# RWKV state update in a two-layer hybrid trunk: both heads' products on the same 64 partitions, and one VectorE instruction that writes the state

## Chip, cores and metric

The kernel runs on one core of one Trainium2 chip. The metric is the device time of one execution in microseconds, the median of the runs shown; smaller is better.

## What is computed

The program is a trunk of two layers over 256 context and 1024 latent tokens of width 1024. The part that the change touches is group C of each token mixer, an RWKV-7 scan: four heads of width 64, two directions, each scan starting on the context tokens and going on over the latent ones. For one head and direction the reference does this for each token:

```python
def wkv_scan(w, k, v, kk, a, s0, reverse, r):
    def update(S, w_t, k_t, v_t, kk_t, a_t):
        sa = jnp.einsum('bhvk,bhk->bhv', S, kk_t)
        return (S * w_t[:, :, None, :] - sa[..., None] * (kk_t * a_t)[:, :, None, :]
                + v_t[..., None] * k_t[:, :, None, :])
    def step(S, x):
        S = update(S, *x[1:])
        return S, jnp.einsum('bhvk,bhk->bhv', S, x[0])
    S, y = lax.scan(step, s0, (tm(r),) + xs, reverse=reverse)
```

S is a 64x64 state of one head, w the decay of each of its 64 key columns. The other groups (a gating MLP and windowed attention), the projections and the SwiGLU sub-layer stay as they are.

## The kernel before

Everything is in float32 or in pairs of float32r parts. TensorE writes PSUM; VectorE (DVE) and ScalarE (ACT) read it back. A float32 product of 128x128 stands in the trace as two weight loads (PEld) and two matmuls (PE). One layer goes through input projections with token shifts, attention and the preparation of the scan (lines 576 to 719), the recurrence, and the output projection and SwiGLU. The two recurrences (one in each layer) lie at about 568 to 743 us and 2255 to 2443 us of the span.

The recurrence works on chunks of 64 tokens. There are four chains, one for each pair of heads (two heads, 64 columns each) and direction; each chain has 20 chunks in five groups of four. The main loop (line 1407) goes over 40 units of two chunks. For each turn it emits five kinds of work, each for another unit, so that they overlap: `u0` (line 1229) multiplies keys and queries of a unit, `u1` and `u4` (lines 1247, 1256) turn these into the matrices of the unit, in the tile `t` (in the trace `U`), and `uy` (line 1283) forms the outputs. Only `u5` (line 1270) is sequential from chunk to chunk: it multiplies the tile `ZV` (in the trace `bC`; rows 0 to 63 are the chunk's values, rows 64 to 127 the state, 64 columns for each of the two heads) with a 128x128 block of `t`, multiplies the product with the decay of the chunk, and writes it into rows 64 to 127 of the next chunk's `ZV`. There are 152 such steps, 76 in each layer.

The 128 columns of the block are the two heads, so the product has head 0 in PSUM partitions 0 to 63 and head 1 in 64 to 127, and of the 128 columns of it each head uses its own 64. The decays lie in the tile `pc`, one column for each chunk, head 0 in partitions 0 to 63, head 1 below. `pc` is filled by one small VectorE copy (line 623) for each of the 20 calls of `alpha`. The write of the state is two instructions on two engines:

```python
V.tensor_scalar(nx[:, 0:64], p[0:64, 0:64], pc[0:64, k:k + 1], None, op0=ALU.mult)
S.activation(nx[:, 64:128], p[64:128, 64:128], AF.Copy, scale=pc[64:128, k:k + 1])
```

The PSUM tile of `u5` has one buffer. Beside the loop, generators in two queues (`bg`, line 191) add other work: `rw_out` (normalising the scan's output), and `inverses` (lines 658 to 719, long runs of VectorE work on lines 671 and 673). The framework puts the instructions of each engine in order and adds the waits, so a change in one place also moves neighbours.

Of the kernel before, what the change touches and what calls it, by code (L numbers as in the profile page):

```python
# [10 lines left out]
F32 = mybir.dt.float32  # L11
F32R = mybir.dt.float32r
AF = mybir.ActivationFunctionType
ALU = mybir.AluOpType
# [80 lines left out]
def trunk(ctx: ExitStack, tc: tile.TileContext, x, ctxt, cc, w_mod, pp, w_in, w_out, lng, lnb, sgw, sink,  # L95
          w2, a2, g2, w_gu, w_down, cst, rope, out, dbg=None):
    nc = tc.nc
    V, S, G, T, D = nc.vector, nc.scalar, nc.gpsimd, nc.tensor, nc.sync
# [3 lines left out]
    stp = ctx.enter_context(tc.tile_pool(name="stats", bufs=4))  # L102
# [10 lines left out]
    def alloc(name, dt=F32):  # L113
        i = free.popleft()
        return Slot(sp.tile([128, NTOK], dt, tag=f"s{i}", name=nm(name)), i)
# [14 lines left out]
    def p_t(tag, bufs, n=512):  # L130
        return psum["pool"].tile([128, n], F32, tag=tag, name=nm(tag), bufs=bufs)
# [15 lines left out]
    def mm(o, lhsT, rhs, start=True, stop=True, parts=False):  # L147
        T.matmul(o, lhsT=lhsT, rhs=rhs, start=start, stop=stop, skip_group_check=parts)  # L148
# [4 lines left out]
        mm(o, a[1], b[0], False, stop, parts)  # L153


    stp.tile([128, 112], F32, name="gap", bufs=1)
    K = cp.tile([128, CSTW], F32, name="cst_sb")
    PP = cp.tile([128, L * PPW], F32, name="pp_sb")
    cs_ = alloc("silu")
# [78 lines left out]
    def wget(ahead=2, slots=False):  # L238
        if not ready:
            emit_w(slots)  # L240
        r = ready.popleft()
        while len(ready) < ahead and plan and plan[0]:
            emit_w(slots)
        return r
# [295 lines left out]
    def layer(l):  # L540
# [19 lines left out]
        V.tensor_scalar(hw[:, 12:14], p_(l, 99, 2), -1.0, 2.0, op0=ALU.mult, op1=ALU.add)  # L560
        rd = dr.tile([3, 128, NTOK], F32, name=f"rd{l}")
        rk = dr.tile([2, 2, 128, 5, 768], F32, name=f"rk{l}")
        pc = stp.tile([128, 80], F32, tag="pc", name=f"pc{l}", bufs=1)
        vt = dr.tile([2, NTOK, 256], F32, name=f"vt{l}")
        cb = dr.tile([4, 5, 128, 1024], F32, name=f"cb{l}")
        td = dr.tile([4, 128, NTOK], F32, name=f"td{l}")
# [9 lines left out]
        def alpha(pair, gi):  # L576
# [9 lines left out]
            lw, Pt = t65(L1.t[:, 0:520]), t65(L1.t[:, 520:1040])  # L586
# [5 lines left out]
            for c, src in ((0, "wd"), (256, "ad")):  # L592
                for d in range(2):
                    lo, _ = gi_slice(d, gi)
                    hd = slice(64 * d, 64 * d + 64)
# [14 lines left out]
            for d in range(2):  # L610
                V.tensor_tensor_scan(L1.t[:, 520 + 260 * d:780 + 260 * d], dm, L1.t[:, 260 * d:260 * d + 260], 0.0,
                                     op0=ALU.mult, op1=ALU.add)
# [7 lines left out]
            V.scalar_tensor_tensor(bh, bh, 0.5, Pi, op0=ALU.mult, op1=ALU.mult)  # L620
            V.tensor_tensor(at, lw[:, :, 0:64], at, op=ALU.mult)
            yield AC
            V.tensor_copy(pc[:, 40 * pair:40 * pair + 40].rearrange("p (d g c) -> p d g c", d=2, c=4)[:, :, gi, :],
                          lw[:, :, 64].rearrange("p (d c) -> p d c", d=2))
            V.tensor_tensor(kh, kh, tk, op=ALU.mult)
            yield AC
            V.tensor_tensor(kh, kh, Pi, op=ALU.mult)
# [93 lines left out]
        def alphas():  # L721
            for pair in range(2):
                while ("kk", pair) not in rw or ("r", pair) not in rw:
                    yield
                for gi in range(5):
                    yield from alpha(pair, gi)
                rw["alpha", pair] = True
# [178 lines left out]
        for n_, i in enumerate(MIXT[3:]):  # L906
# [3 lines left out]
            w, raw, dst = wget(), alloc("raw"), alloc("mx")  # L910
# [309 lines left out]
        def unit(ci, gi, c):  # L1220
            g = grp[ci, gi]
            m = (ci * 10 + gi * 2 + c // 2) % len(UR)
            t = UR[m].t[:, 0:1024].rearrange("p (j w) -> p j w", w=512)
            return g, t, g["c0"], [z[:, c * 256:c * 256 + 512].rearrange("p (j w) -> p j w", w=256) for z in g["H"]]
# [45 lines left out]
        def u5(ci, gi, c, j):  # L1270

            if gi == 4 and c + j == 3:
                return
            g, t, c0, _ = unit(ci, gi, c)
            c += j
            p = p_t("u5", PB["u5"])
            mm(p[:, 0:128], t[:, j, 256:384], g["ZV"][:, c * 128:(c + 1) * 128])
            nx = g["ZV"][64:128, (c + 1) * 128:(c + 2) * 128] if c < 3 else grp[ci, gi + 1]["ZV"][64:128, 0:128]
            k = g["pc"] + c
            V.tensor_scalar(nx[:, 0:64], p[0:64, 0:64], pc[0:64, k:k + 1], None, op0=ALU.mult)  # L1280
            S.activation(nx[:, 64:128], p[64:128, 64:128], AF.Copy, scale=pc[64:128, k:k + 1])

        def uy(ci, gi, c):
            g, t, c0, _ = unit(ci, gi, c)
# [122 lines left out]
        for n in range(len(ul) + LAG):  # L1407
            if n % 2 == 1 and n // 2 + 2 < len(gl):
                beta_load(*gl[n // 2 + 2])
            if n % 2 == 0:  # L1410
                own()
            s5, s4, s1, s0 = (at(n, lag) for lag in (LAG, 2, 1, 0))

            if s5:
                u5(*s5, 0)
            if s4:
                u4(*s4)
            if s1:
                u1(*s1)
            if s5:  # L1420
                u5(*s5, 1)
            if n < len(ul) + 1:
                bg(4 if n >= len(ul) - 4 else 2)
            bg(2 * EL_B, 1)
            if s0:
                u0(*s0)
            if s5:
                uy(*s5)
                ci, gi, c = s5
                if chains[ci][0] == 1 and c == 2 and gi in (0, 2, 4) and (full or gi):  # L1430
                    bgq.append(rw_out(chains[ci][1], {0: 0, 2: 2, 4: 1}[gi]))
            if n >= len(ul) - 12 and n % 2 == 1 and len(ready) < WR:
                emit_w(len(ready) >= 1)
            if n == len(ul) - 6 or (full and n == len(ul) - 4):
                GB[len(GB)] = gb_tile(l, 0, len(GB))
# [401 lines left out]
        for f in range(NCL, NFF):  # L1837
            w = side.pop()
# [111 lines left out]
    for n, (src, a, b) in enumerate(list(plan)[:16]):  # L1950
        w = alloc("wraw")
# [25 lines left out]
    for l in range(L):  # L1977
        layer(l)
# [33 lines left out]
```

## Time and profile before

| | |
|---|---|
| median of 3 runs | 3242.0 us (3241.93 to 3243.32) |
| the profiled execution | 3247.78 us, span 3246.0 us |
| busy PE, PEld, DVE, ACT, POOL | 3112.2, 2568.5, 1966.6, 1361.2, 525.7 us |
| the two recurrences (560 to 745, 2250 to 2445 us) | PE busy 334.36 of 380 us, DVE 248.84, ACT 221.23 |
| mean granted TensorE clock | 0.984 of full speed |

The profile is of one execution. Busy times add up the records of an engine; a matmul's record includes its way through the array, so that records of matmuls that follow each other overlap. PEld is the loading of weights, which can lie beside a matmul. A row's number in brackets is the idle time of its engine just before it and what ended it. Line 148 is the helper `mm` through which nearly all products go, so products are told apart by their tiles.

### The profile page before, as it was taken

What the parts mean: (1) busy time and instruction counts of PE and PEld (TensorE: products, weight loads), DVE (VectorE), ACT (ScalarE), POOL (GpSimd) and SP (SyncE); (2) the same over time, 40 slices, a digit from 0 to 9 for tenths busy, and PEclk for the clock granted to TensorE, in tenths of its full rate; (3) what the DMA queues carried; (4) which work ended last, traced back from release to release, by engine and by line L of the source; (5) the groups of instructions that cost most, each with busy time, mean ns of one, the idle gap of its engine ahead of it and who ended that gap; (6) DMA issues with size and microseconds to landing.
All of it is one profiled execution on the core that took longest, in us unless ns stands there. A gap on an engine that the chain in (4) does not pass through costs nothing.

```text
span 3246.0 us, 49544 instructions
## 1 busy us (share of the span) xinstructions
PE 3112.2 (96%) x18980; PEld 2568.5 (79%) x18980; DVE 1966.6 (61%) x3654; ACT 1361.2 (42%) x2634; POOL 525.7 (16%) x604
## 2 busy tenths in 40 slices
PE   7999999999999999999999999999888999999998
PEld 4868877886788888886687788887776788887886
DVE  3448877665465555554455657886655656666556
ACT  4455567564332222232112556576454422324211
POOL 2300101232102222200001220112121122331000
PEclk8999999999999999999999999999999999999999
DMA  6477222446512222145622357313445122223322
GB/s 224 141 238 246 80 75 85 125 126 225 194 41 65 72 70 70 64 144 194 244 86 91 113 177 235 125 55 103 120 116 212 67 73 90 78 85 130 107 95 98
DMA packets 411166, 403.82 MB, mean 124 GB/s; under 512 B 134576, under 2 KB 350640, under 8 KB 410928
## 3 DMA queue, kind: packets, MB, share of 16 engines
q1 hardware_dynamic: 410928, 400.65, 38.4%
q8 instruction: 150, 2.46, 0.3%
q14 instruction: 88, 0.72, 0.1%
HBM read 279.97 MB, written 120.59 MB: 123 GB/s over the span
## 4 chain that ended last, share of the span: by engine, by line
PE 73%; DVE 9%; DMA 4%; ACT 3%; issue 3%; POOL 1%; SPq 1%; DVEq 0%; POOLq 0%; ACTq 0%
PE dd L148 26%; PE mm L148 21%; PE xx L148 17%; PE u L148 4%; PE mm L1132 1%; DMA wm<-in_w_mod 1%; PE xx L1132 1%; DVE eL L671 1%; DVE eX L673 1%; PE gg L148 1%; SPq L648 1%; DVE bC L1245 1%; DVE yac L1745 0%; DMA ao<-rk 0%; DMA ar<-actd 0%
## 5 line engine op out<-in xcount | busy, mean ns | idle before, releaser
L148 PE MATMUL mm<-h,wh 128*128 128x512 f32 (+1 forms) x1424 | 423.5, 380 | 2.7 <-ACT ntmp L402 2.3
L148 PE MATMUL dd<-h,wh 128*128 128x256 f32 (+1 forms) x1312 | 323.3, 338 | 2.8 <-DVE h L411 1.6
L148 PE MATMUL mm<-wh,h 128*128 128x256 f32 x1472 | 324.6, 296 | 1.3 <-ACT gel L872 0.6
L148 PEld LDWEIGHTS mm<-h,wh 128*128 128x128 f32 x1424 | 260.2, 191 | 62.1 <-issue 13.7
L148 PE MATMUL mm<-h,wl 128*128 128x512 f32 (+1 forms) x712 | 267.5, 376 | 1.1 <-DVE wl L233 1.1
L148 PEld LDWEIGHTS mm<-wh,h 128*128 128x128 f32 x1472 | 247.8, 193 | 18.7 <-issue 14.6
L148 PEld LDWEIGHTS dd<-h,wh 128*128 128x128 f32 x1312 | 228.9, 192 | 30.9 <-DVE h L411 2.1
L1623 ACT ACTIVATE wh<-wq 128x1024 fp32r<-128x1024 f32 x114 | 121.0, 1061 | 303.6 <-PE dd L148 113.9
L148 PE MATMUL dd<-h,wl 128*128 128x256 f32 (+1 forms) x656 | 220.2, 336 | 0.0
L148 PE MATMUL mm<-wl,h 128*128 128x256 f32 x736 | 210.3, 286 | 0.1
L1624 DVE TENSOR_TENSOR wl<-wq,wh 128x1024 fp32r<-128x1024 f32 x114 | 140.3, 1231 | 115.6 <-ACT wh L1623 115.6
L180 POOL TENSOR_TENSOR ss<-ss,mh_sb 128x1 f32<-128x1 f32 x74 | 50.5, 683 | 860.1 <-DVE ss L379 859.3
L148 PE MATMUL dd<-tt,wh 128*128 128x512 f32 x608 | 188.2, 391 | 0.0
L148 PEld LDWEIGHTS mm<-h,wl 128*128 128x128 f32 x712 | 136.2, 191 | 25.3 <-DVE wl L233 1.4
L1745 DVE TENSOR_TENSOR yac<-yac,mm 128x512 f32<-128x512 f32 x126 | 86.3, 685 | 107.6 <-PE mm L148 107.5
L148 PEld LDWEIGHTS mm<-wl,h 128*128 128x128 f32 x736 | 142.1, 193 | 2.0 <-issue 1.4
L1745 DVE TENSOR_TENSOR yac<-yac,xx 128x512 f32<-128x512 f32 x126 | 86.2, 684 | 91.7 <-PE xx L148 91.6
L1613 POOL TENSOR_TENSOR wq<-wu 128x512 f32<-128x512 f32 x38 | 49.1, 1293 | 561.7 <-DVE wl L1624 477.7
L148 PEld LDWEIGHTS dd<-h,wl 128*128 128x128 f32 x656 | 125.4, 191 | 12.5
L148 PEld LDWEIGHTS dd<-tt,wh 128*128 128x128 f32 x608 | 111.8, 188 | 21.2
L148 PE MATMUL dd<-tt,wl 128*128 128x512 f32 x304 | 118.4, 389 | 0.0
L1098 ACT ACTIVATE P<-P,nmx 128x640 f32<-128x640 f32 (+2 forms) x144 | 109.0, 759 | 16.6 <-DVE nmx L1093 16.6
(373 smaller groups left out, 7674.2 us busy)
## 6 DMA issues: line engine op xcount, KB each, us to landing
wm<-in_w_mod SPq DMA_DIRECT2D x80, 512.0 KB, 5.0
wr<-in_w_down SPq DMA_DIRECT2D x44, 512.0 KB, 4.5
wr<-in_w_in SPq DMA_DIRECT2D x38, 512.0 KB, 4.9
cb<-ao SPq DMA_DIRECT2D x76, 256.0 KB, 2.8
wu<-in_w_gu SPq DMA_DIRECT2D x38, 512.0 KB, 3.7
wq<-in_w_gu SPq DMA_DIRECT2D x38, 512.0 KB, 3.7
ao<-rk SPq DMA_DIRECT2D x58, 256.0 KB, 3.9
xs<-xr SPq DMA_DIRECT2D x28, 512.0 KB, 2.6
```

The source lines that it names most:

```text
L148: T.matmul(o, lhsT=lhsT, rhs=rhs, start=start, stop=stop, skip_group_check=parts)
L180: G.tensor_tensor(dst, src, mh[:, :n], op=ALU.pow)
L648: D.dma_start(Ld[base:base + 16].rearrange("(c h z) i j -> h (z i) c j", h=2, z=2)[h], ld_[64 * h:64 * h + 64, 4 * d:4 * d + 4])
L671: V.tensor_tensor(tmp, Lm[:, j + 1:, j:j + 1].to_broadcast([n, r, c]), X[:, j:j + 1, :c].to_broadcast([n, r, c]), op=ALU.mult)
L673: V.tensor_tensor(X[:, j + 1:, :c], X[:, j + 1:, :c], tmp, op=ALU.subtract)
L1098: S.activation(po, po, AF.Exp, scale=0.125, bias=nmx[:, i:i + 1], accum_out=sm[:, i:i + 1])
L1132: T.transpose(ps[:, z * 128:(z + 1) * 128], P[i // 2].t[:, c:c + 128], ident)
L1245: V.tensor_tensor(C[h][oh, :, 0:128], p[oh, :, 0:128], two(mLK[oh], 128), op=ALU.mult)
L1613: G.tensor_tensor(a[:, 0:512], u[:, 0:512], u[:, 512:1024], op=ALU.add)
L1623: S.activation(w.hi[i], raw[i], AF.Copy)
L1624: V.tensor_tensor(w.lo[i], raw[i], f32(w.hi[i]), op=ALU.subtract)
L1745: V.tensor_tensor(yac[t].t[:, c], yac[t].t[:, c], ps, op=ALU.add)
```

## The change

`u5` now makes two products, one for each head: 64 columns of the block as weights, 64 columns of `ZV` as the moving side, both into PSUM partitions 64 to 127, side by side. The decays of both heads are kept in partitions 64 to 127 of `pc`, which is twice as wide (an unused tile of the same pool is made narrower by the same 80 columns). One VectorE multiplication of 64x128 with the decay broadcast over the 64 columns of each head writes the state. The ScalarE instruction is gone. `alpha` fills `pc` with two copies in place of one.

```diff
-    stp.tile([128, 112], F32, name="gap", bufs=1)
+    stp.tile([128, 32], F32, name="gap", bufs=1)
...
-        pc = stp.tile([128, 80], F32, tag="pc", name=f"pc{l}", bufs=1)
+        pc = stp.tile([128, 160], F32, tag="pc", name=f"pc{l}", bufs=1)
...
-            V.tensor_copy(pc[:, 40 * pair:40 * pair + 40].rearrange("p (d g c) -> p d g c", d=2, c=4)[:, :, gi, :],
-                          lw[:, :, 64].rearrange("p (d c) -> p d c", d=2))
+            for h in range(2):
+                V.tensor_copy(pc[64:128, 80 * h + 40 * pair:80 * h + 40 * pair + 40].rearrange("p (d g c) -> p d g c", d=2, c=4)[:, :, gi, :],
+                              lw[64 * h:64 * h + 64, :, 64].rearrange("p (d c) -> p d c", d=2))
...
-            mm(p[:, 0:128], t[:, j, 256:384], g["ZV"][:, c * 128:(c + 1) * 128])
+            for h in range(2):
+                mm(p[64:128, 64 * h:64 * h + 64], t[:, j, 256 + 64 * h:320 + 64 * h], g["ZV"][:, c * 128 + 64 * h:c * 128 + 64 * h + 64])
             nx = g["ZV"][64:128, (c + 1) * 128:(c + 2) * 128] if c < 3 else grp[ci, gi + 1]["ZV"][64:128, 0:128]
             k = g["pc"] + c
-            V.tensor_scalar(nx[:, 0:64], p[0:64, 0:64], pc[0:64, k:k + 1], None, op0=ALU.mult)
-            S.activation(nx[:, 64:128], p[64:128, 64:128], AF.Copy, scale=pc[64:128, k:k + 1])
+            w = pc[64:128, :].rearrange("p (h k) -> p h k", h=2)[:, :, k:k + 1]
+            hd = "p (h v) -> p h v"
+            V.tensor_tensor(nx.rearrange(hd, h=2), p[64:128, 0:128].rearrange(hd, h=2), w.to_broadcast([64, 2, 64]), op=ALU.mult)
```

The rows below show where instructions stand, with their waits; `u0`, `u1`, `u4`, `u5` and `uy` are the PSUM tiles of the helpers of that name, `bC3` is `ZV`, `pc0` is `pc`, and sizes are those of the output. First TensorE in layer 0, around two steps of the state, before:

```order
L148 MATMUL u5_947_6674<-bC3_908_6329,U_903_6305 128x128 [waits DMAHW0_49,Activation_49]
L148 MATMUL u1_949_6685<-U_905_6307,bC_844_6014 128x128 [waits DMAHW7_49,DMAHW6_49,DVE_49]
L148 MATMUL u1_949_6685<-U_905_6307,bC_844_6014 128x128
L148 MATMUL u0_951_6694<-bC_844_6014,bC_843_6013 128x128
L148 MATMUL uy_952_6702<-U_903_6305,bC3_908_6329 128x128 [waits PE_49]
L148 MATMUL u0_957_6729<-bC_856_6064,bC_855_6063 128x128 [waits DMAHW5_49,DMAHW6_49,DMAHW4_49,DVE_49]
L148 MATMUL u5_950_6690<-bC3_908_6329,U_903_6305 128x128 [waits Activation_49]
L148 MATMUL uy_952_6702<-U_903_6305,bC3_908_6329 128x128
```

and with the change, at the same place:

```order
L148 MATMUL u5_947_6684<-bC3_908_6339,U_903_6315 64x64 [waits DMAHW0_49,DVE_49]
L148 MATMUL u5_947_6684<-bC3_908_6339,U_903_6315 64x64
L148 MATMUL u0_951_6704<-bC_844_6024,bC_843_6023 128x128 x2
L148 MATMUL u1_949_6695<-U_905_6317,bC_844_6024 128x128 [waits DMAHW7_49,DMAHW6_49,DVE_49]
L148 MATMUL u1_949_6695<-U_905_6317,bC_844_6024 128x128
L148 MATMUL uy_952_6712<-U_903_6315,bC3_908_6339 128x128 [waits PE_49,Activation_49]
L148 MATMUL u0_957_6739<-bC_856_6074,bC_855_6073 128x128 [waits DMAHW5_49,DMAHW6_49,DMAHW4_49,DVE_49]
L148 MATMUL u0_957_6739<-bC_856_6074,bC_855_6073 128x128
L148 MATMUL u5_950_6700<-bC3_908_6339,U_903_6315 64x64 [waits DVE_49]
L148 MATMUL u5_950_6700<-bC3_908_6339,U_903_6315 64x64
L148 MATMUL uy_952_6712<-U_903_6315,bC3_908_6339 128x128
```

Each step is a pair of 64x64 products that follow each other, with products of 128x128 on both sides; it waits for VectorE where it waited for ScalarE. Seven products stand between these two steps in place of five. Second, ScalarE at the same place, before:

```order
L1265 ACTIVATE U_904_6306<-u4_948_6678 128x2x128 [waits PE_49,Activation_49]
L1254 ACTIVATE bC_841_6011<-u1_949_6685 64x2x128 [waits PE_49]
L1281 ACTIVATE bC3_908_6329<-u5_947_6674,pc0_258 64x64 [waits DVE_49]
L1254 ACTIVATE bC_842_6012<-u1_949_6685 64x2x128
L1302 ACTIVATE Y_896_6290<-uy_952_6702 64x128 [waits PE_49]
L1302 ACTIVATE Y_896_6290<-uy_952_6702 64x128
L1281 ACTIVATE bC3_908_6329<-u5_950_6690,pc0_258 64x64 [waits DVE_49]
L1265 ACTIVATE U_905_6307<-u4_954_6713 128x2x128 [waits PE_49,Activation_49]
```

and with the change:

```order
L1266 ACTIVATE U_904_6316<-u4_948_6688 128x2x128 [waits PE_49,Activation_49]
L1255 ACTIVATE bC_841_6021<-u1_949_6695 64x2x128 [waits PE_49]
L1255 ACTIVATE bC_842_6022<-u1_949_6695 64x2x128
L1305 ACTIVATE Y_896_6300<-uy_952_6712 64x128 [waits PE_49]
L1305 ACTIVATE Y_896_6300<-uy_952_6712 64x128
L1266 ACTIVATE U_905_6317<-u4_954_6723 128x2x128 [waits PE_49,Activation_49]
```

Before, each write of head 1 (line 1281) waited for VectorE, that is, for the write of head 0, although it uses other columns; with the change ScalarE has no part in the state any more.

## Rows read from the trace of the kernel before

**Rows 1.** Stretches of the recurrences: length, PE, PEld, DVE, ACT, POOL busy, clock, DMA.

```profile
560.00:745.00 185.00, 169.01 (x1413) 149.81 (x1409) 125.54 (x325) 115.82 (x331) 55.21 (x71) 1.00 0.47 128
2250.00:2445.00 195.00, 165.35 (x1402) 144.67 (x1394) 123.30 (x321) 105.41 (x302) 44.47 (x56) 0.96 0.48 131
```

**Rows 2.** Instructions of the tile bC: count, ns minimum/median/maximum, first and last start.

```profile
L1280 DVE TENSOR_SCALAR bC<-u,pc x152: 276/277/279, 577.1 to 2441.7; 64x64 f32<-64x64 f32 x152
L1281 ACT ACTIVATE bC<-u,pc x152: 296/308/311, 577.4 to 2442.3; 64x64 f32<-64x64 f32 x152
```

**Rows 3.** Line 1281: what ScalarE idled for before it, then who waited for it.

```profile
  DVE bC L1280: 36.5, 59
...
  PEld u L148: 28.9, 60
  PE u L148: 12.5, 29
  PEld uy L148: 3.0, 3
```

**Rows 4.** Timeline, 640.4 to 641.5 us: start, length, engine, line; a waiting step.

```profile
640.57 0.28 DVE L1280 TENSOR_SCALAR bC<-u,pc 64x64 f32<-64x64 f32 x1
...
640.88 0.31 ACT L1281 ACTIVATE bC<-u,pc 64x64 f32<-64x64 f32 x1 [0.66 <-DVE bC L1280]
...
641.24 0.30 PEld L148 LDWEIGHTS u<-bC,U 128*128 128x128 f32 x2 [0.23 <-ACT bC L1281]
```

**Rows 5.** Timeline, 2329.3 to 2329.7 us: weight loads of a step without wait.

```profile
2329.43 0.30 PEld L148 LDWEIGHTS u<-bC,U 128*128 128x128 f32 x2
...
2329.65 0.19 PEld L148 LDWEIGHTS uy<-U,bC 128*128 128x128 f32 x1
```

**Rows 6.** Timeline, 2308.6 to 2309.3 us: a 32*32 product between a step and uy.

```profile
2308.63 0.30 PEld L148 LDWEIGHTS u<-bC,U 128*128 128x128 f32 x2 [1.03 <-ACT bC L1281]
2308.64 0.49 PE L148 MATMUL u<-bC,U 128*128 128x128 f32 x2 [0.84 <-ACT bC L1281]
...
2309.05 0.13 PEld L148 LDWEIGHTS gg<-jT 32*32 32x32 f32 x2
...
2309.22 0.19 PEld L148 LDWEIGHTS uy<-U,bC 128*128 128x128 f32 x1
```

**Rows 7.** Timeline, 506 to 507.4 us: attention's 128*64 products between products of 128*128.

```profile
506.62 0.65 PE L148 MATMUL xx<-PT,Vt 128*64 128x256 f32 x4
507.21 0.30 PEld L148 LDWEIGHTS dd<-kl,qs 128*128 128x128 f32 x2 [0.39 <-issue]
```

**Rows 8.** Timeline, 163.7 to 165.6 us: the weight loads of 16 products of 64*64.

```profile
164.10 1.01 PEld L148 LDWEIGHTS xx<-ao 64*64 64x64 f32 x32 [0.35 <-issue]
```

**Rows 9.** Groups by line and shape: VectorE multiplications that read PSUM, by size.

```profile
L1245 DVE TENSOR_TENSOR bC<-u,cst_sb 64x256 f32<-64x256 f32 x160 | 67.5, 422 | 4.2
...
L959 DVE TENSOR_TENSOR kt<-mm,rope 128x128 f32<-128x128 f32 x16 | 4.5, 278 | 3.2 <-ACT Vt L973 3.2
```

**Rows 10.** The tile pc: the copies that fill it.

```profile
L623 DVE COPY pc<-al x20: 155/164/173, 160.3 to 2058.5; 128x8 f32<-128x8 f32 x20
```

**Rows 11.** Stretches 570 to 590, 2255 to 2305 us: sum; line 1281 alone.

```profile
sum 70.00, PE 63.11 PEld 57.76 DVE 65.11 ACT 34.48 POOL 11.20; mean PE 31.55 PEld 28.88 DVE 32.55 ACT 17.24 POOL 5.60
...
570.00:590.00 20.00, 2.13 (x7) 1.00 0.39 101
2255.00:2305.00 50.00, 6.74 (x22) 1.00 0.42 108
```

**Rows 12.** Waits of the weight loads in these two stretches: us, times, longest.

```profile
PEld u L148 <- ACT bC L1281: 0.6, 2, 0.4
...
PEld u L148 <- ACT bC L1281: 5.4, 10, 1.4
```

**Rows 13.** Timeline, 442.3 to 443.4 us: transposes marked 128*64 after a 128*128 product.

```profile
442.46 0.41 PE L148 MATMUL mm<-wh,h 128*128 128x256 f32 x2
...
442.66 0.38 PEld L1005 LDWEIGHTS xx<-cst_sb,kt 128*64 128x64 f32 x4
```

## The prediction, as it went on record

> **What bounds the kernel now.** I read the busy times by stretch first. In the two recurrences TensorE is busy for 169.0 of 185 and 165.4 of 195 us [rows 1]: it is nearly full, but 46 us of the 380 are idle. VectorE and ScalarE have room over the whole stretch. Then I asked whom TensorE waits for. The state's second write, line 1281 on ScalarE, is the name to look for: weight loads waited for it 63 times, 28.9 + 3.0 = 31.9 us together, and matmuls of u 12.5 us [rows 3]. The timeline shows why. VectorE writes head 0 (0.28 us from 640.57), ScalarE starts head 1 at 640.88, when VectorE has ended, takes 0.31, and the next product's weights start at 641.24 [rows 4]. ScalarE idled 36.5 us in 59 such handovers [rows 3]. So the chain of a step is product, VectorE, ScalarE, product, and the change cuts one link out of it.
>
> **What the link is worth.** ScalarE's 0.308 us [rows 2] and one handover of 0.03 (640.85 to 640.88) [rows 4] make 0.34 us in each step that waits. A step that does not wait gains nothing. A wait costs a little more than its row says: in a stream the weight loads of a step and the next product are 0.22 apart for two loads [rows 5], 0.11 each, though one load takes 0.19, so the load would have started 0.08 before the last one ended. 63 waits are worth 31.9 + 63 x 0.08 = 37 us, 0.59 each on average. That is the most that the chain can give back.
>
> The new VectorE instruction covers 128 columns in place of 64. Rows of the same operation from PSUM give 0.278 us for 128 columns and 0.422 for 256 [rows 9]; the old one takes 0.277 [rows 2]. I take 0.28, nothing added; the upper bound of 0.42 would take 0.14 of the 0.34 back, 63 x 0.14 = 9 us in all; the row of the same size is the nearest. ScalarE loses 152 x 0.308 = 47 us of work, which was not a bound. The second copy into pc adds 20 x 0.164 = 3.3 us at most to VectorE [rows 10], before the recurrence, beside projections; nothing, or 3 us if that cover is gone.
>
> **What the two half products cost.** This is the term that decides. A step was one 128*128 product, two loads 0.11 apart, 0.22 us [rows 5]. Now it is two products with 64 weight columns, four loads. Sixteen 64*64 products with 32 loads took 1.01 us, 0.03 per load, but there two parts of the array alternate [rows 8]; in one and the same part I take twice that, 4 x 0.06 = 0.24 us. The products alone add 0.02.
>
> Around them, however, the array changes its division, from 128*128 to 128*64 and back. The trace has this change in other places, and there the overlap of loads is lost. In one place a 32*32 product stands between a step and uy [rows 6]: its load starts at 2309.05, 0.08 before the step's record ends (2308.64 + 0.49), and uy's load at 2309.22, 0.59 after the step's first load, against 0.22 without it [rows 5]. The detour costs 0.37 us. The small product's own two loads are worth some 0.06 [rows 8], so two changes of division cost 0.31. Attention's 128*64 products, the same division as the new ones, show the same at their end: the next 128*128 load starts at 507.21 while the last record ends at 507.27 (506.62 + 0.65) [rows 7]. A step without a wait therefore becomes 0.31 + 0.02 = 0.33 us longer, and 152 steps cost 50 us. The bounds are 0.31 and 0.37 for a step, 47 and 56 us.
>
> The Trainium skill has this as a rule that speaks against the change: TensorEngine Tiling (Array Packing), Key Properties, says that switching the tiling mode, not merely the tile, drains the engine. The loads that start only as the last record ends [rows 6, 7] agree with it; by the rule the sum below stands, and without it the term of 50 us would go and the change would gain.
>
> **The sum.** In a step that waited, the chain comes 0.34 earlier and TensorE itself 0.33 later; that covers waits of up to 0.67 - 0.08 = 0.59, and the mean row is 31.9/63 = 0.51. Some are longer (up to 1.4 [rows 12]), and I leave 5 us for them, an estimate. So 37 - 5 = 32 us come back and 50 are added: +18.
>
> Two things take off from that. Where inverses runs beside the recurrence, VectorE is busy 65.1 of 70 us [rows 11] and sets the pace. 29 steps lie there (7 + 22), with 12 waits of 6.0 us [rows 11, 12]: 29 x 0.33 = 9.6 added, 6.0 + 1.0 given back, and TensorE has the slack for the difference: 2.6 us fall out, +15. And TensorE's other idle time, 46 - 13 = 33 us in the recurrences [rows 1, 3], waits for transfers, GpSimd and rw_out's chains, most of which do not run through a step; a TensorE that comes later waits less for them. I take a fifth, 7 us, an estimate: **+8 us**. The order also helps a little there: seven products now stand between the two steps shown above in place of five.
>
> The sum is made against the profiled execution, 3247.8 us, which becomes 3256; the median of the runs lies 5.8 us lower. I predict **3250 us**, 0.25% above 3242.0. A measurement of this kernel tells 0.2%, 6.5 us, from no change.
>
> **Rivals.**
> 1. *Nothing that can be told* (3236 to 3248). The same terms, with more of the idle time soaked up: nearly half of the 33 us in place of a fifth makes +15 - 15 = 0. For it: ScalarE, relieved of 47 us, also writes U and bC earlier. Against it: idle time behind uy and u0 is not all in the steps' way.
> 2. *Faster: the array does not change its division in a costly way.* The point that decides is whether the first load of a half product may lie beside the product before it. For it: the transposes of line 1005 carry the mark 128*64 too, and their load starts at 442.66, 0.21 before the record of the 128*128 product before them ends (442.46 + 0.41) [rows 13]. Against it: they are transposes, and true products show the gap [rows 7]. Then a step costs 0.02, 3 us, the waits give 37 - 7 = 30 (without VectorE's stretch): -27, 3215 us. With half the price of the two changes, 0.16, a step costs 0.18, 27 us, and 32 come back, less 7 of other idle time: -12, 3230 us.
> 3. *Much slower: loads in one part of the array do not overlap.* If the four loads keep 0.11 each [rows 5], a step grows by a further 4 x 0.11 - 0.24 = 0.20, 30 us in all: +38, 3280 us. For it: no row has two such products after each other in one part with a short moving side. Against it: 0.06 for each part where two alternate [rows 8].
>
> A page names rival 3's mechanism: TensorE: Matmul & The Clock Gate, The mechanism, says in the Trainium skill that a load overlaps a running product only when their row groups differ, and the two halves share all rows. The trace does not agree for whole products: 0.11 apart with 0.19 for a load [rows 5].
>
> **How the numbers follow.** The forecast's own case, +7 to +28 us, has 0.46; rival 1 has 0.28; rival 2 has 0.18, of which 0.08 for the full price and 0.10 for the half; rival 3 has 0.08. Faster by over 0.2% is rival 2, 0.18; the same is rival 1, 0.28; slower is the rest, 0.54. The range leaves out the full case of rival 2 and rival 3: its low end is the half case, 3230 us, and its high end, 3270 us, is the forecast's case with 0.37 for a step (56 - 32 = +24, nothing soaked up) and the 3.3 us of the copies; the forecast with VectorE's upper bound, 8 + 9 = +17, lies inside. The likeliest case alone runs from 3249 to 3270.
>
> **What would show it.** Right: loads of u with 128*64 that start as the record before them ends, and a gap of the same kind behind them, named "issue"; some 0.55 us from a step's first load to the next product's where it was 0.22; weight loads that wait for the new VectorE instruction (line 1284) some 5 to 10 us in all; line 1267, which waits for ScalarE's U, less idle; recurrences together some 8 us longer than 380, all else the same. Wrong: half products that lie in the stream at 0.06 apart with no gap (rival 2), or 0.11 apart (rival 3), or a total wait for line 1284 that is near the old 32 us, which would say that VectorE's queue and not the second link held the state back.

## The result, and the profile after

The kernel with the change takes 3277.8 us (median of 4 runs, 3275.9 to 3279.6) against 3242.7 of the kernel before on the same chip: a ratio of 1.0106, 95% interval 1.0094 to 1.0118, **35 us slower**. The forecast had the sign and missed the size: 3250 us with a range of 3230 to 3270. The profiled execution took 3277.1 us, 29.3 more than the one of before (3247.8).

First the page, whose columns are busy time, share of the span and instructions:

```profile
span 3275.3 us, 50109 instructions
...
PE 3141.8 (96%) x19284; PEld 2581.6 (79%) x19284; DVE 1975.8 (60%) x3674; ACT 1317.1 (40%) x2482; POOL 525.9 (16%) x604
```

To see where the 29 us lie, I use the matmuls of uy, the outputs of the recurrence, as marks. The tile uy in the trace of before, layer by layer; the columns are count, ns (least, median, most), first and last start in us, forms:

```profile
L148 PE MATMUL uy<-U,bC x160: 272/275/377, 576.7 to 742.8; 128*128 128x128 f32 x160
...
L148 PE MATMUL uy<-U,bC x128: 273/275/378, 2266.4 to 2442.9; 128*128 128x128 f32 x128
```

The same view of after:

```profile
L148 PE MATMUL uy<-U,bC x160: 272/275/421, 580.5 to 763.6; 128*128 128x128 f32 x160
...
L148 PE MATMUL uy<-U,bC x128: 273/275/377, 2297.1 to 2475.6; 128*128 128x128 f32 x128
```

Before the first mark 3.8 us are lost (576.7 to 580.5). The first recurrence grows from 166.1 to 183.1 us, the second from 176.5 to 178.5: 19.0 us together. Between them lie 9.9 us more, and 3.4 come back after the last mark. From here on, "the recurrences" are these two stretches from mark to mark, 342.6 us before and 361.6 after. One caution goes with them: the framework does not put the last uy of the first layer at the same place in every kernel, so where that matters the first layer is also counted to a later mark, the first projection behind the recurrence (the product mm from wm,c).

The step itself went as its mechanism was forecast. The timeline of after's weight loads, a step that waits for nothing (start, length, engine, line):

```profile
590.64 0.30 PEld L148 LDWEIGHTS u<-bC 128*128 128x128 f32 x2
591.06 0.31 PEld L148 LDWEIGHTS u<-bC,U 128*64 128x64 f32 x4
591.44 0.30 PEld L148 LDWEIGHTS uy<-U,bC 128*128 128x128 f32 x2
```

And the product before it, in the matmuls of the same timeline:

```profile
590.75 0.39 PE L148 MATMUL u<-bC 128*128 128x128 f32 x2
```

The record before the step ends at 591.14, and the half products' first load starts at 591.06, 0.08 before that, as it did at the 32*32 product of [rows 6]. The four loads are done in 0.31, 0.06 apart, and the next product's load comes 0.38 after the step's first, where two whole loads took 0.22 [rows 5]. The tile bC shows all 152 steps:

```profile
L148 PEld LDWEIGHTS u<-bC,U x608: 132/138/231, 577.8 to 2473.5; 128*64 128x64 f32 x152
...
L1284 DVE TENSOR_TENSOR bC<-u,pc x152: 294/295/296, 581.0 to 2474.8; 64x128 f32<-64x128 f32 x152
```

The state's one write takes 0.295 us, against 0.277 + 0.308 for the two [rows 2]. The view of [rows 3] says who waited for the write (us, times). Before, it has one more line:

```profile
  PE uy L148: 2.4, 2
```

and of line 1284, after, it shows:

```profile
  PEld u L148: 2.9, 6
  PE u L148: 1.7, 4
  PEld uy L148: 0.6, 2
  PE uy L148: 0.2, 1
```

Weight loads (PEld) wait 3.5 us where they waited 31.9; the matmuls themselves (PE) stand idle for it 1.9 us where it was 12.5 + 2.4 = 14.9. The chain's waits are gone, and the recurrences are longer all the same. The windows from mark to mark say how (busy us and, in brackets, instructions of each engine, granted clock, DMA share, GB/s); before:

```profile
576.70:743.10 166.40, 154.37 (x1298) 138.11 (x1296) 108.14 (x283) 107.00 (x310) 48.93 (x60) 1.00 0.47 130
2266.40:2443.20 176.80, 149.94 (x1194) 130.11 (x1192) 111.16 (x285) 95.72 (x276) 41.13 (x51) 0.96 0.46 127
sum 343.20, PE 304.31 PEld 268.22 DVE 219.30 ACT 202.72 POOL 90.06; mean PE 152.16 PEld 134.11 DVE 109.65 ACT 101.36 POOL 45.03
```

and after:

```profile
580.50:763.90 183.40, 170.57 (x1440) 146.23 (x1438) 109.10 (x280) 84.16 (x232) 44.42 (x57) 0.98 0.41 111
2297.10:2475.90 178.80, 160.57 (x1334) 136.40 (x1332) 107.51 (x280) 73.17 (x200) 38.75 (x49) 0.96 0.43 117
sum 362.20, PE 331.14 PEld 282.63 DVE 216.60 ACT 157.33 POOL 83.17; mean PE 165.57 PEld 141.31 DVE 108.30 ACT 78.67 POOL 41.59
```

TensorE is busy for 26.8 us more and idle for 7.8 us less (343.2 - 304.3 = 38.9 before, 362.2 - 331.1 = 31.1 now). So 13 us of idle time for the state went, and only 8 of all idle time: some 5 came back in waits for other things. The 28 us by which the waits of weight loads fell are no measure of this, since a load can wait while the record of the product before it still runs.

### The profile page after: what moved, and what is told of

It is laid out like the page before. It is cut to its first block, busy times and chain, and to the rows that moved or that the text cites. A ratio compares the mean times of both kernels' runs of the same rounds, so it can differ in the third digit from the quotient of the medians.

```text
span 3275.3 us, 50109 instructions
## 1 busy us (share of the span) xinstructions
PE 3141.8 (96%) x19284; PEld 2581.6 (79%) x19284; DVE 1975.8 (60%) x3674; ACT 1317.1 (40%) x2482; POOL 525.9 (16%) x604
## 4 chain that ended last, share of the span: by engine, by line
PE 76%; DVE 7%; DMA 3%; ACT 3%; issue 2%; POOL 1%; SPq 1%; DVEq 0%; POOLq 0%; ACTq 0%
PE dd L148 26%; PE mm L148 21%; PE xx L148 17%; PE u L148 6%; PE mm L1133 1%; PE uy L148 1%; PE xx L1133 1%; PE gg L148 1%; DMA ao<-rk 1%; SPq L649 1%; DVE yac L1748 0%; POOL ss L180 0%; DVE mx L483 0%; DVE xr L1777 0%; POOL hr L180 0%
## 5 line engine op out<-in xcount | busy, mean ns | idle before, releaser
L148 PEld LDWEIGHTS mm<-h,wl 128*128 128x128 f32 x712 | 135.9, 191 | 24.6 <-DVE wl L233 1.4
```

## The experiments

In all of them "recurrences" is measured as above, and the ratio is to the kernel before on the same chip.

**e1_full_width: no change of the division.** The change, but each half product takes 128 weight columns, 64 of them only to fill (columns of U set to zero once, or the other head's); the state's rows come out on the same partitions.

```diff
-  mm(p[64:128, 64*h:64*h+64], t[:, j, 256+64*h:320+64*h], g["ZV"][:, c*128+64*h:c*128+64*h+64])
+  mm(p[:, 64*h:64*h+64], t[:, j, 192+64*h:320+64*h], g["ZV"][:, c*128+64*h:c*128+64*h+64])
...
+  for u in UR:
+      G.memset(u.t[:, 0:1024].rearrange("p (j w) -> p j w", w=512)[:, :, 192:256], 0.0)
```

> The change, but each of the two products has 128 weight columns (64 unused ones and one head's 64), so that the array never changes its division in a step; the state is still written by the one VectorE instruction. The 64 unused columns of U are set to zero once. Division theory (two changes of division cost 0.36 us in each of 152 steps, 54 us): these go, four whole loads of 0.11 in place of two cost 0.22 a step, 33 us, and the waits that the change removed, some 33 us, stay removed: about 3245 us, within 0.5% of the kernel before and 25 to 35 us faster than the change. Order theory (the new order of neighbours costs the time): 3265 to 3280. Product theory (two products in a step cost it, however they lie): 3270 to 3285.

Measured: 1.0040 [1.0026, 1.0054], 3256.0 us. The tile uy:

```profile
L148 PE MATMUL uy<-U,bC x160: 272/275/377, 583.3 to 753.1; 128*128 128x128 f32 x160
...
L148 PE MATMUL uy<-U,bC x128: 272/275/421, 2287.8 to 2461.7; 128*128 128x128 f32 x128
```

The recurrences take 169.8 + 173.9 = 343.7 us, 17.9 less than with the change. Over all steps (from the load before a step to its first, and from that to the next product's, medians) an uninterrupted step costs 0.112 + 0.447 = 0.559 us here and 0.313 + 0.375 = 0.688 with the change; 152 x 0.129 = 19.6, close to the 17.9. So the division is what makes the change's step dear, although its loads are the shorter ones. In the whole time e1 is 22 us faster than the change, a little less than was expected, and still 0.40% above the kernel before; by the profiles nearly all of that lies outside the recurrences, and the copies (see e4) can be only part of it.

**e8_double_changes: two more changes of the division in each step.** One whole product, whose result nobody uses, between the two halves.

```diff
   for h in range(2):
+      if h:
+          mm(p[:, 256:320], t[:, j, 256:384], g["ZV"][:, c*128:c*128+64])
       mm(p[64:128, 64*h:64*h+64], ...
```

> The change, with one more product between the two halves of each step: 128 weight columns, 64 moving ones, into unused columns of the same PSUM tile, so that the division of the array changes four times in a step in place of two. Its result is not used. By the price read from the change (0.20 on the way in and 0.16 on the way out beside the loads themselves), the two further changes cost 0.3 to 0.36 us a step and the product's own two loads 0.22: 152 x 0.55 = 84 us over the change, some 3360; less by up to 15 us where TensorE waits anyway. If changes of division cost nothing, the product's 0.22 alone: 33 us, some 3310.

Measured: 1.0331 [1.0309, 1.0353], 3349.4 us. Weight loads of one step in the timeline:

```profile
641.25 0.81 PEld L148 LDWEIGHTS u<-bC,U 128*64 128x64 f32 x6 [0.33 <-ACT bC L1255]
642.13 0.97 PEld L148 LDWEIGHTS u<-bC 128*128 128x128 f32 x8
```

From a step's first load to the next product's load it is 0.88 us, 0.50 more than with the change. The added product's own two loads are 0.22 [rows 5]; 0.28 is left for its two changes. The recurrences take 423.5 us, 62 more than with the change, or 0.41 a step. A change of division costs time in the middle of a step as it does at its ends; rival 2 falls with this and e1.

**e2_split_only: the division without the shorter chain.** The kernel before with its product cut in two, both writes as before. The two halves go to their own PSUM partitions, 0 to 63 and 64 to 127, and not both to 64 to 127 as with the change.

```diff
-  mm(p[:, 0:128], t[:, j, 256:384], g["ZV"][:, c*128:(c+1)*128])
+  for h in range(2):
+      mm(p[64*h:64*h+64, 64*h:64*h+64], t[:, j, 256+64*h:320+64*h], g["ZV"][:, c*128+64*h:c*128+64*h+64])
```

> The kernel before, with its two writes of the state on VectorE and ScalarE; only the product is cut into two of 64 weight columns, one in each half of the array. Division theory: 152 steps with two changes each cost some 0.3 us a step, 45 us, less what the waits for line 1281 soak up: 3270 to 3290 us. Order theory: within 10 us of the kernel before, 3235 to 3252, since the chain of the state is as before. Product theory: 3250 to 3265.

Measured: 1.0075 [1.0058, 1.0091], 3267.4 us. Its tile uy:

```profile
L148 PE MATMUL uy<-U,bC x160: 273/275/417, 574.0 to 756.2; 128*128 128x128 f32 x160
...
L148 PE MATMUL uy<-U,bC x128: 275/275/582, 2281.2 to 2466.2; 128*128 128x128 f32 x128
```

182.2 + 185.0 = 367.2 us, 24.6 more than before, in a kernel whose weight loads still wait 34.7 + 1.5 = 36.2 us for ScalarE's write. The whole time lies between two of the expected ranges. Two things have to be known before this kernel is set against the change. First, its step is cheaper in the stream. Weight loads of one step:

```profile
632.21 0.20 PEld L148 LDWEIGHTS u<-bC,U 128*64 128x64 f32 x4
632.47 0.30 PEld L148 LDWEIGHTS uy<-U,bC 128*128 128x128 f32 x2
```

The halves lie in two parts of the array, their loads go two at a time, 0.007 us apart, and the next product's load comes 0.265 after the step's first (median) where it is 0.375 with the change: 0.11 a step, up to 17 us in 152. An uninterrupted step costs 0.313 + 0.265 = 0.578, 0.25 more than before. Second, the end of the first layer lies otherwise. Matmuls:

```profile
751.72 0.49 PE L148 MATMUL uy<-U,bC 128*128 128x128 f32 x2
755.12 1.08 PE L523 MATMUL gg<-cst_sb,gsq 128*128 128x128 f32 x4 [2.91 <-DVE gsq L519]
756.00 0.63 PE L148 MATMUL uy<-U,bC 128*128 128x128 f32 x2
...
761.03 1.07 PE L148 MATMUL mm<-wm,c 128*32 128x512 f32 x8
```

The last uy stands behind the norm's transposes (line 523) and their wait of 2.9 us, which in the kernel before and with the change come after it. From the first uy to the projection the first layer takes 175.3 us before, 187.1 here and 197.6 with the change. So counted, the split alone costs 11.8 + 8.5 = 20.3 us in the two layers, not 50, and the change is 10.5 us longer than e2 in the first layer and 6.5 shorter in the second. That is the net of a shorter chain, of halves that lie one behind the other, and of another order at the end; no run separates the three.

**e3_two_vector: both writes on VectorE.** The kernel before, without the second engine in the chain.

```diff
-  S.activation(nx[:, 64:128], p[64:128, 64:128], AF.Copy, scale=pc[64:128, k:k+1])
+  V.tensor_scalar(nx[:, 64:128], p[64:128, 64:128], pc[64:128, k:k+1], None, op0=ALU.mult)
```

> The kernel before, but both writes of the state are VectorE instructions of 64x64; the product is whole. No change of division. If the second link on ScalarE (its start after VectorE, its 0.31 us and its queue) is what TensorE waited for, most of the 32 us of waits remain only as far as 0.28 us in place of 0.34 and ScalarE's queue go: 3222 to 3240 us. If VectorE's queue held the state, nothing is gained and VectorE has 42 us more to do: 3242 to 3260.

Measured: 1.0018 [1.0007, 1.0029], 3249.8 us; recurrences 171.2 + 175.3 = 346.5, 3.9 longer. Here too the last uy stands behind the norm's transposes and their wait; to the projection the first layer is 1.6 us longer than before and the second 1.2 shorter. Taking ScalarE out of the chain gives nothing while two instructions remain: the second VectorE write takes 0.290 us where ScalarE took 0.308 [rows 2]. The time falls into the second of the two expected cases, but the change's 3.5 us of waits speak against its reason, that VectorE's queue holds the state back.

**e5_all_narrow and e9_narrow_two_writes: the chain's worth when the division is free.** In both, every product of the recurrence (u0, u1, u4, uy) is cut into halves of 64 weight columns like the step's, so nothing in it changes the division. e5 is the change with this; e9 is e2 with this, so the two writes stay.

```diff
+  def mmh(o, lhsT, rhs):
+      for h in range(2):
+          mm(o[64*h:64*h+64], lhsT[:, 64*h:64*h+64], rhs)
...
-  mm(p[:, j, c0:128], g["Ti"][:, (c+j)*128:(c+j)*128+128], t[:, j, c0:128])
+  mmh(p[:, j, c0:128], g["Ti"][:, (c+j)*128:(c+j)*128+128], t[:, j, c0:128])
```

> The change, with every product of u0, u1, u4 and uy also made in two halves of 64 weight columns (the two halves of the array side by side; for uy only the part of each head that is used), so that a step of the state stands between products of the same division. Division theory: the 54 us go, two halves side by side take no longer than a whole product (0.03 us a load where two parts alternate), and the waits stay removed: 3205 to 3230 us, faster than the kernel before. Product theory: twice the number of products in the recurrence cost 60 us or more: over 3300. Order theory: no forecast, about the change's 3278.

> All products of the recurrence in halves of 64 columns, as in the run that made them so, but the state written by VectorE and then ScalarE as in the kernel before, with head 0 and head 1 in their own halves of PSUM. No change of division in either run, so the two differ in the chain of the state alone. If the cut in the chain is worth the 30 us that the waits for line 1281 showed: 3265 to 3280 us, 15 to 30 slower than the run with one write. If TensorE's other waits take the place of those for the state: within 8 us of it, 3240 to 3255.

Measured: e5 1.0019 [1.0008, 1.0029], 3251.2 us; e9 1.0013 [1.0003, 1.0023], 3248.3 us. The recurrences of e5 take 171.3 + 168.1 = 339.4 us, 22 less than with the change and 3 less than before. Those of e9:

```profile
L148 PE MATMUL uy<-U,bC x320: 218/222/369, 575.4 to 749.0; 128*64 128x64 f32 x160
...
L148 PE MATMUL uy<-U,bC x256: 218/222/368, 2270.2 to 2446.0; 128*64 128x64 f32 x128
```

173.6 + 175.8 = 349.4 us, 10 more than e5's. But as in e2 the last matmuls of uy, eight of them, stand behind the norm's transposes and a wait of 3.5 us, and in e5 before them. To the projection the first layer takes 177.8 us in e9 and 183.9 in e5, so that e5 is 6.1 us longer there, 7.7 shorter in the second layer, and 1.6 shorter together. The two also differ in more than the chain: e9's halves of a step lie in two parts of the array, e5's in one. Narrow products throughout free the change of its division. What the shorter chain gains in the second layer is given up at the end of the first, and nothing of it is seen in the whole time, where e5 stands 3 us above e9 and both above the kernel before; the 3205 to 3230 us expected of e5 were missed by over 20 us.

**e4_copies_only: the second copy into pc.** The kernel before with pc of 160 columns and two copies of 64 partitions.

```diff
-  V.tensor_copy(pc[:, 40*pair:40*pair+40]..., lw[:, :, 64]...)
+  for h in range(2):
+      hp = slice(64*h, 64*h+64)
+      V.tensor_copy(pc[hp, 40*pair:40*pair+40]..., lw[hp, :, 64]...)
```

> The kernel before, with only what the change does outside the recurrence: pc twice as wide (the unused tile narrower) and filled by two copies of 64 partitions in place of one of 128. The step of the state is as before. If these copies and what they move among their neighbours cost the 10 us that the change lost outside its recurrences: 3250 to 3256 us, the loss lying before the first recurrence and before the second. If not: within 3 us of the kernel before, and the 10 us belong to the new steps' effect on the order.

Measured: 1.0013 [1.0005, 1.0022], 3249.0 us: 5.3 us between the medians and 4.2 by the ratio, for 20 instructions more; this lies between the two cases that were expected. The recurrences keep their length, 342.2. Set beside before, the same matmuls come 3.6 us later at 224 us and 7.0 later at 453, where the first of these figures varies between executions and the growth of 3.4 is what the stretch itself adds. In the six profiles with two copies (the change, e1, e4, e5, e8, e10) this growth is 1.9 to 4.7 us, in the six with one (e2, e3, e9 and, below, e6, e7, e11) -0.3 to 1.3. The windows of before show that there is little room: where many of these copies run, VectorE is nearly full.

```profile
260.00:325.00 65.00, 62.78 (x533) 55.96 (x532) 59.38 (x138) 35.91 (x69) 1.57 (x6) 1.00 0.74 234
```

The third busy time of this row of the windows is VectorE's: 59.4 of 65 us. TensorE, the first, is busy for 62.8.

**e6_late_copy and e11_late_copy_again: the change with one copy as before.** alpha writes one copy of 128 partitions; head 0's half is moved once in a layer, ahead of the recurrence. e10_change_again is the change itself, on the chip of e11.

```diff
-  for h in range(2):
-      V.tensor_copy(pc[64:128, 80*h+40*pair:80*h+40*pair+40]..., lw[64*h:64*h+64, :, 64]...)
+  V.tensor_copy(pc[:, 80+40*pair:80+40*pair+40]..., lw[:, :, 64]...)
...
+  V.tensor_copy(pc[64:128, 0:80], pc[0:64, 80:160])
```

> The change, but pc is filled by one copy of 128 partitions in each alpha as in the kernel before, and head 0's decays are brought to partitions 64 to 127 by one copy for each layer at the start of the recurrence. If the second copies cost the 10 us outside the recurrences: 10 us faster than the change, about 3265 to 3270, recurrences as in the change. If not: 3275 to 3281, as the change. Division theory by itself: the recurrences stay 19 to 27 us longer than before in either case.

> The change itself again, beside the kernel before on the same chip, as the base for the next run: ratio to the kernel before 1.009 to 1.012.

> The change with the single late copy of the decays again, on the same chip as the change: if the second copies in alpha cost the 5 us that they cost in the kernel before, 4 to 6 us faster than the change (ratio to the kernel before lower by 0.0012 to 0.002); if the loss outside the recurrences comes with the new steps and the order of the other work, no difference beyond 2 us.

Measured: e6 1.0101 [1.0083, 1.0119], 3272.4 us (runs of 3269.9 to 3284.3); e10 1.0117 [1.0102, 1.0132], 3280.7 us; e11 1.0085 [1.0072, 1.0099], 3269.4 us. So one copy saves 11 us beside e10 on the same chip, where 4 to 6 or nothing was expected. Between e6 and the first measurement of the change it is 5, not clear of the noise. The recurrences are the same, 361.2 us in e10 and 361.6 in e11. From 208 to 453 us e6's lag behind before grows by 0.8 us (3.2 to 4.0), where e4's grew by 3.4 from 224 on. How many of the 11 us are the copies is less sure than that they lie outside the recurrences: the profiles of e6 and e11, which are one kernel, start the first recurrence at 580.9 and 574.8 us, and most of that difference is there by 208 us, ahead of VectorE's full stretch.

**e7_narrow_late: e5 and the late copy together**, the version without either cost.

```diff
-  mm(p[:, j, c0:128], ...
+  mmh(p[:, j, c0:128], ...
...
+  V.tensor_copy(pc[64:128, 0:80], pc[0:64, 80:160])
```

> All products of the recurrence in halves of 64 columns (as in the run that made them so) and the single late copy of the decays. If the copies cost 6 to 10 us outside: 3238 to 3245 us, the same as the kernel before or faster, with recurrences 4 us shorter than before; if they do not: about 3251, as that run.

Measured: 1.0002 [0.9993, 1.0011], 3244.8 us; recurrences 171.9 + 167.9 = 339.8 us. It is the kernel before's equal, and no version that was run is faster than it.

The recurrences side by side, in us, with the first layer also counted to the projection behind it; e6, e10 and e11 are as the change to 0.5 us, e7 as e5 to 0.6:

| kernel | state's writes | division changed | first | first, to the projection | second | first and second | ratio |
|---|---|---|---|---|---|---|---|
| before | 2 | no | 166.1 | 175.3 | 176.5 | 342.6 | 1 |
| e4 | 2 | no | 166.6 | 175.8 | 175.6 | 342.2 | 1.0013 |
| e3 | 2 | no | 171.2 | 176.9 | 175.3 | 346.5 | 1.0018 |
| e9 | 2 | no, all narrow | 173.6 | 177.8 | 175.8 | 349.4 | 1.0013 |
| e2 | 2 | yes | 182.2 | 187.1 | 185.0 | 367.2 | 1.0075 |
| the change | 1 | yes | 183.1 | 197.6 | 178.5 | 361.6 | 1.0106 |
| e1 | 1 | no, all whole | 169.8 | 179.8 | 173.9 | 343.7 | 1.0040 |
| e5 | 1 | no, all narrow | 171.3 | 183.9 | 168.1 | 339.4 | 1.0019 |
| e8 | 1 | twice | 210.3 | 223.0 | 213.2 | 423.5 | 1.0331 |

## Why the prediction was wrong

**Right: the mechanism and its price in the stream.** The division changes, the overlap of the loads is lost on both sides, and an uninterrupted step costs 0.688 - 0.33 = 0.36 us more (0.20 ahead of it, 0.16 behind), where 0.33 was forecast and 0.37 was the upper bound. The Trainium skill's rule, TensorEngine Tiling (Array Packing), Key Properties, is that switching the tiling mode drains the array. This trace agrees, with the half products' first load 0.08 us before the end of the record ahead of them. VectorE's write takes 0.295 us for 0.28, four loads in one part take 0.31 in all, so rival 3 falls too (that its 3280 us lie 2 us from the measured time is chance), and the state's waits are down to 3.5 us, under the 5 to 10 that were forecast.

**Right in size, in part by luck: "32 us come back and 50 are added: +18".** Up to the last uy the recurrences grew by 19.0, up to the projection by 24.5, so how well +18 fits depends on the mark. By the price in the stream 152 x 0.36 = 54 us were added, and 35 or 30 of them came back. That is near the forecast's two terms, but it is an estimate, and the 32 were put down to the chain alone. e2 has the long chain, owes 152 x 0.25 = 38 us by its own price and shows 24.6 or 20.3: some 13 to 18 us vanish in waits that are there anyway. What is left for the shorter chain is then some 12 to 22 us, an estimate too; the most that two runs set side by side show as a net gain is 6.5 us (e2 and the change) and 7.7 (e9 and e5), in the second layer, where the waits were long (20.0 of the 31.9 us); in the first layer, to the projection, the same pairs lose 10.5 and 6.1. And of the 13.0 us that TensorE stood idle for the state, 5 returned as other idle time (13.0 less 7.8); waits of u's loads for U, for example, grew from 0.3 and 0.5 us in the two layers to 2.3 and 3.7 (line 1265, now 1266).

**Wrong: "Two things take off from that", 3 and 7 us.** This is the step that failed in the recurrences: they grew by 19.0 us where +8 was forecast, 11 us of the miss, of which the price of 0.36 in place of 0.33 makes some 4. In the stretches that VectorE fills, where on balance nothing was to be added, the lag of the change against before grew as elsewhere, by 2 us in 570 to 590 and by 3 in 2250 to 2300. A likely reason, which is argued and not shown: what other idle time soaks up is already within the 35 us that came back, and it was taken off a second time on the difference.

**Wrong: the copies into pc, "nothing, or 3 us if that cover is gone".** I named TensorE's projections as the cover. The copies run on VectorE, and it was nearly full itself (the row of 260 to 325 us under e4). e4 puts a cost of 4 to 5 us on the edit (1.6 to 7.1 by its interval); the time that the copies last, 20 x 0.17 = 3.4 us, lies inside it. So the upper value of the forecast fits, and zero does not.

**Missed: the end of the first recurrence.** From the last uy to the projection the kernel before needs 9.4 us and the changed one 14.6. Matmuls in the timeline, before:

```profile
742.60 0.49 PE L148 MATMUL uy<-U,bC 128*128 128x128 f32 x2 [0.49 <-ACT bC L1281]
745.14 1.09 PE L523 MATMUL gg<-cst_sb,gsq 128*128 128x128 f32 x4 [2.06 <-DVE gsq L519]
...
751.99 1.93 PE L148 MATMUL mm<-wm,c 128*32 128x512 f32 x8
```

and after:

```profile
763.53 0.38 PE L148 MATMUL uy<-U,bC 128*128 128x128 f32 x2
765.86 1.05 PE L148 MATMUL gg<-cst_sb,gsq 128*128 128x2 f32 x8 [1.94 <-ACT gsq L1331]
771.29 1.08 PE L523 MATMUL gg<-cst_sb,gsq 128*128 128x128 f32 x4 [4.38 <-DVE gsq L519]
...
778.15 1.94 PE L148 MATMUL mm<-wm,c 128*32 128x512 f32 x8
...
785.48 0.63 PE L148 MATMUL dd<-wl,mhi 128*128 128x512 f32 x1
...
789.21 0.39 PE L148 MATMUL dd<-wsh,mlo 128*128 128x512 f32 x1
```

The sums of the norm (gg from gsq, eight matmuls of 128x2) were done before the last uy in the kernel before, at 740.50 us; now they stand behind it, with a wait of 4.4 us after them, and some matmuls behind it take 0.63 us in place of 0.39, at a granted clock of 0.52 (785 to 788.5 us), the lower level, after a stretch in which TensorE was busy for 7.4 of 15.5 us. At a product common to both, 37 us behind before's last uy (mm from wm,c, at 780.14 before and 808.47 after), the lag is 28.3 us, 7.5 more than at the last uy. My prediction looked at the order inside the recurrence and not at what it leaves over. In e10 and e11 the same wait of 4.4 us stands there, in e5 and e7 one of 4.0 without a change of division, in e4 that of 2.1 as before; no run changes the tail alone, so that it follows from the order of the new steps is only argued.

**Wrong by 5 us: the median below the profile.** The 5.8 us between before's profiled execution and its median were taken off again; the profile of after (3277.1) lies at its median. That is scatter between executions and no mechanism.

In the profiles, then: 19.0 in the recurrences, 7.5 at the first one's end, 3.8 ahead of it, 2.4 between that end and the second, 3.4 returned behind it: 29.3 us, where +8 was forecast. The likeliest case lay on the right side, but its own range, 3249 to 3270, took the copies at 3.3 us as their worst and had no term for what the new order leaves behind.

## What to carry to other kernels

A product of half the width can cost more than a whole one: here, narrowing one product in a stream was paid for on both sides by the division of the array, and the price went when all neighbours were narrowed or the product was filled up to full width. Neither made the kernel faster than before. A wait that is removed from a chain, and a cost that is added, are worth their rows only where that chain or that engine sets the pace; a kernel with one part of the edit alone tells each term, if it changes nothing else in the stream, and a soaked-up share must be taken off once. A stretch is measured between marks that keep their place in the order: 10 us between e9 and e5 were 1.6 by a better mark. Before an instruction is costed at nothing, read how full its own engine is in that very stretch, not the engine that works beside it.

## What the hardware showed that was not expected

The price of a change of the division was expected from a 32*32 product, which costs 0.31 for two changes; a pair of 128*64 products of the same kernel costs 0.36 where both lie in one part of the array, 0.25 where each has its own (e2), and a whole product between two halves 0.28 for its two. Loads of 64 weight columns follow each other at 0.06 us into one and the same part; into two parts they go in pairs, 0.007 apart (e2), so that each part again gets one every 0.06. The Trainium skill, TensorE: Matmul & The Clock Gate, The mechanism, lets a load overlap a running product only where row groups differ. The two halves share all rows, and the 0.06 do not agree with that sentence; they do not speak against the section's opening, by which a load into the background weight buffer may go ahead as well.
